# Forming one weight sum of the seven-product pairs with an accumulating DMA, and using eight such pairs per group

## The chip, the core and the metric

The kernel runs on one core of a Trainium2 chip. The core has a matrix engine (TensorE, "PE" in the profile; "PEld" is its weight load), three engines for elementwise work (VectorE, "DVE"; ScalarE, "ACT"; GpSimd, "POOL"), a queue that issues transfers (SyncE, "SP") and 16 DMA engines between HBM and the on-chip memory SBUF. TensorE adds up its results in PSUM, eight banks of 512 columns. The metric is the device time of one execution in microseconds.

## The reference

One layer of a hybrid decoder, batch 1, 256 tokens and 16 meta tokens in front, model width 4096, all in float32:

```python
h = rmsnorm(x, norm_g)
p = h @ w_in                      # 4096 x 16384: q, k, v, gate | B, C, h, z
o = stick_breaking_attention(heads(q), heads(k), heads(v))
o = group_rmsnorm(o * silu(g_attn), attn_norm_g, 16)
y = b_conv * short_conv(c_conv * h_conv, conv_w)
y = group_rmsnorm(y * silu(z_conv), conv_norm_g, 16)
return rmsnorm(x + concatenate([o, y]) @ w_out, final_norm_g)[:, 16:]
```

Almost all the arithmetic is in the two matrix products. The output keeps the 256 real tokens.

## The kernel before

**Three matmuls for one product.** TensorE multiplies in a rounded format (float32r). To keep float32 accuracy every operand is split: ScalarE casts it to the rounded format (`wh`, line 282), VectorE subtracts that from the original (`wl`, line 283), and a product is three matmuls: low x high, high x high, high x low (lines 314, 316 and 317 in `mm_p`).

**Groups and pieces.** The input projection goes through eight groups of two heads each. The list `pieces` sets the order of the work. In a group come first 16 pairs (j = 0 to 15). A pair covers two blocks of 128 rows of the weights, and has two pieces of 128 x 1024, called A and B. With W1 and W2 for the columns of q and gate, and of B and z, in the two blocks, A holds W1 of the first block and W2 of the second, B the opposite. After the pairs come 32 pieces "p" for k, v, C and h (lines 306 to 308), with the attention and convolution of the group as tasks between. After all groups the output projection follows (pieces "o", lines 705 to 707).

**Seven products in place of eight.** A pair stands for a 2 x 2 block product: two blocks of tokens times two of rows, and two sets of columns: eight block products of 512 columns, 24 matmuls. For the pairs in `SJ` (in groups 1 to 7) a scheme of the Strassen-Winograd kind does with seven products, 21 matmuls. It needs sums of the token blocks (`S`, formed once, in group 0, by `prep_x`, lines 207 to 216: four GpSimd operations, a ScalarE copy, a VectorE subtraction) and sums of the weight blocks, formed anew in each group: T (1024 columns, two sums of 512) and U (two more, written over A in its buffer). So such a pair has four pieces, A, B, T and U, of 6, 3, 6 and 6 matmuls. The products go to eight PSUM banks, and `evict_sums` (lines 479 to 491) adds them up after the last pair of `SJ`.

**What runs ahead.** At step i the program has issued loads up to piece i + 8 and splits up to piece i + 5. What holds them back are buffers: five for loaded pieces (`raw`), six for splits (`wh`, `wl`), one for T (`tt`). All loads stand in SyncE's queue in order, all casts in ScalarE's and all subtractions in VectorE's, so a waiting instruction holds what stands behind it. A scheduler orders the instructions of each engine when the program is built; it may put a load or a sum some places earlier than the code has it.

**T and U before.** When B of such a pair is split, VectorE forms T with two subtractions of 512 columns (line 293) and U with an addition and a subtraction (294, 295).

Of the kernel before, what the change touches and what calls it, by code (L numbers as in the profile page):

```python
# [37 lines left out]
WARM = 10  # L38
LOADS, SPLITS, RING = 8, 5, 6

SJ = (4, 6, 8, 10, 12, 14)


G0, CW0, AG0, CG0, NPAR = 0, 32, 80, 96, 112
# [3 lines left out]
def kernel(ctx, tc, xt, xin, xm, par, fg, w1, w2, out):  # L48
# [141 lines left out]
    def prep_x(j, parts=1):  # L190
        t = xr.pop(j)
        x = xs[j // 2][:, 2 * (j % 2):2 * (j % 2) + 2, :, :L]
        for i in range(2):
            g = pt[:, G0 + 2 * j + i:G0 + 2 * j + i + 1]
            if i or parts == 2:
                nc.vector.tensor_scalar(out=t[:, i, :], in0=t[:, i, :], scalar1=g, scalar2=None, op0=ALU.mult)
            else:
                nc.scalar.mul(out=t[:, i, :], in_=t[:, i, :], mul=g)
            if parts == 2:
                nc.scalar.copy(out=x[:, i, 0, :], in_=t[:, i, :])  # L200
                nc.vector.tensor_tensor(out=x[:, i, 1, :], in0=t[:, i, :], in1=x[:, i, 0, :].bitcast(F32), op=ALU.subtract)
        if parts == 1:
            nc.scalar.copy(out=x[:, :, 0, :], in_=t)
            nc.vector.tensor_tensor(out=x[:, :, 1, :], in0=t, in1=x[:, :, 0, :].bitcast(F32), op=ALU.subtract)
        if j not in SJ:
            return
        a11, a21 = t[:, 0, META:META + P], t[:, 0, META + P:]
        a12, a22 = t[:, 1, META:META + P], t[:, 1, META + P:]
        f = wk.tile([P, 4, P], F32, tag="u2", name=f"sf{j}", bufs=2)
        v = nc.gpsimd  # L210
        v.tensor_tensor(out=f[:, 0, :], in0=a21, in1=a22, op=ALU.add)
        v.tensor_tensor(out=f[:, 2, :], in0=a11, in1=a21, op=ALU.subtract)
        v.tensor_tensor(out=f[:, 1, :], in0=f[:, 0, :], in1=a11, op=ALU.subtract)
        v.tensor_tensor(out=f[:, 3, :], in0=a12, in1=f[:, 1, :], op=ALU.subtract)
        nc.scalar.copy(out=S[j][:, 0], in_=f)
        nc.vector.tensor_tensor(out=S[j][:, 1], in0=f, in1=S[j][:, 0].bitcast(F32), op=ALU.subtract)

# [12 lines left out]
    def load(i):  # L230
        p = pieces[i]
        if p[0] in "TU":
            return
        if p[:2] == ("A", 0) and p[2] > 0:
            load_x(p[2])
        t = wp.tile([P, 1024], F32, tag="raw", name=f"raw{i}", bufs=5)
        raws[i] = t
        if p[0] == "x":
            if p[1] < 8:
                r, c = divmod(p[1], 4)  # L240
                nc.sync.dma_start(out=t, in_=xin[r * P:(r + 1) * P, c * 1024:(c + 1) * 1024])
            else:
                nc.sync.dma_start(out=t[:, :512], in_=xm)
        elif p[0] == "m":
            nc.sync.dma_start(out=t.rearrange("p (a b) -> p a b", a=4), in_=mixd[p[1]])
        elif i < 2:
            for h in range(2):
                nc.sync.dma_start(out=t[:, 512 * h:512 * h + 512], in_=where[i][:, 512 * h:512 * h + 512])
                if i == 0 and h == 0:
                    nc.sync.dma_start(out=xr[0][:, 1:, :], in_=xt[:, 1:2, :])  # L250
        else:
            nc.sync.dma_start(out=t, in_=where[i])
# [3 lines left out]
    def split(i):  # L256
        p = pieces[i]
        if p[:2] == ("A", 0):
            prep_x(p[2], 2 if p[2] == 0 else 1)
        parts = 2 if i < 2 else 1  # L260
        if p[0] == "x":
            t = raws.pop(i)
            w = 1024 if p[1] < 8 else 512
            nc.scalar.activation(out=t[:, :w], in_=t[:, :w], func=AF.Square, accum_out=sq9[:, p[1]:p[1] + 1])
            return
        if p[0] == "m":
            t = raws.pop(i).rearrange("p (a b) -> p a b", a=4)
            h, lo = mixh[p[1]], mixl[p[1]]
            nc.scalar.copy(out=h, in_=t)
            nc.vector.tensor_tensor(out=lo, in0=t, in1=h.bitcast(F32), op=ALU.subtract)  # L270
            return
        t = sums.pop(p) if p[0] in "TU" else raws.pop(i)
        two = p[0] in "AB" and p[1] and p[2] in SJ
        w = 512 if two and p[0] == "B" else 1024
        if i in keep:
            h, lo = keep[i]
        else:
            h = wp.tile([P, 1024], F32R, tag="wh", name=f"wh{i}", bufs=RING)
            lo = wp.tile([P, 1024], F32R, tag="wl", name=f"wl{i}", bufs=RING)
        for q in range(parts):  # L280
            c = slice(q * w // parts, (q + 1) * w // parts)
            nc.scalar.copy(out=h[:, c], in_=t[:, c])  # L282
            nc.vector.tensor_tensor(out=lo[:, c], in0=t[:, c], in1=h[:, c].bitcast(F32), op=ALU.subtract)  # L283
        splits[i] = (h, lo)
        if two and p[0] == "A":
            sums[p] = t
        elif two:

            a = sums.pop(("A",) + p[1:])
            s = wp.tile([P, 1024], F32, tag="tt", name=f"t{i}", bufs=1)  # L290
            for q in range(2):
                c = slice(512 * q, 512 * q + 512)
                nc.vector.tensor_tensor(out=s[:, c], in0=a[:, c], in1=t[:, 512:], op=ALU.subtract)
            nc.vector.tensor_tensor(out=a[:, 512:], in0=a[:, 512:], in1=s[:, :512], op=ALU.add)
            nc.vector.tensor_tensor(out=a[:, :512], in0=t[:, :512], in1=a[:, 512:], op=ALU.subtract)
            sums[("T",) + p[1:]], sums[("U",) + p[1:]] = s, a


    psum = {}
# [179 lines left out]
    def evict_sums(g):  # L479

        cq = wk.tile([P, 2, 512], F32, tag="cq", name=f"cq{g}")
        cb = wk.tile([P, 2, 512], F32, tag="cb", name=f"cb{g}")
        gr[g] = dict(cq=cq, cb=cb)
        if g == 0:
            return
        p1, p5, p7, p6 = (psum.pop((g, q)) for q in (P1, P5, P7, P6))
        A.copy(out=cq[:, 0], in_=p1)
        V.tensor_tensor(out=cb[:, 0], in0=p6, in1=cq[:, 0], op=ALU.add)
        V.tensor_tensor(out=cq[:, 1], in0=p7, in1=cb[:, 0], op=ALU.add)
        V.scalar_tensor_tensor(out=cb[:, 0], in0=p5, scalar=-1.0, in1=cb[:, 0], op0=ALU.mult, op1=ALU.add)  # L490
        V.scalar_tensor_tensor(out=cb[:, 1], in0=p5, scalar=-1.0, in1=cq[:, 1], op0=ALU.mult, op1=ALU.add)

    def evict(g):
        s = gr[g]
# [186 lines left out]
    def load_res(nb):  # L681
        c, w = cols(nb)
        for t in range(2):
            nc.sync.dma_start(out=res[t][:, c:c + w], in_=xin[t * P:(t + 1) * P, c:c + w])
        f = fgs["pool"].tile([P, 512], F32, tag="fg", name=f"fg{nb}", bufs=2)
        nc.sync.dma_start(out=f[:, :w], in_=fg[:, c:c + w].broadcast_to([P, w]))
        fgs[nb] = f

# [169 lines left out]
```

## Time and profile before

| | |
|---|---|
| time, median of 3 runs | 1837.21 us (1837.15 to 1838.44) |
| profiled execution | 1838.6 us, span from first to last instruction 1836.7 us |
| granted TensorE clock | 0.997 of full speed |
| HBM | read 354.48 MB, written 7.86 MB, 197 GB/s over the span |
| group 0: pairs | about 7 to 96 us |
| groups 1 to 7: one each | some 182 us, of which the pairs take about 83 |
| output projection and end | from 1472.8 us |

The profile is one execution. "Busy" is the time in which an engine worked on at least one instruction; matmuls overlap, so their durations add up to more than that. A row such as `L283 DVE TENSOR_TENSOR wl<-raw,wh` names the line of the kernel, the engine, the operation and the tiles written and read. In the rows in order of time the first two columns are the start and the duration in microseconds, and a bracket says how long the engine stood idle before and what released it.

### The profile page before, as it was taken

The numbers are of one execution on the slowest core, as the hardware profiler recorded it, in microseconds if no ns is written. First come the engines' busy times: TensorE is split into PE (matmuls) and PEld (weight loads), VectorE is DVE, ScalarE is ACT, GpSimd is POOL, SyncE is SP. The second block draws the span as 40 slices with busy tenths as digits, with TensorE's granted clock in tenths as the row PEclk, the third lists the DMA queues.
The fourth block names the chain that finished last, engine by engine and source line by source line (L and its number), as shares of the span: only waits on it lengthen the run. The fifth ranks groups of instructions, "written<-read, shape, count | busy, mean of one in ns | idle before, by whom it ended". The sixth has DMA issues, their size and how long they took to land.

```text
span 1836.7 us, 29147 instructions
## 1 busy us (share of the span) xinstructions
PE 1822.2 (99%) x11196; PEld 1646.2 (90%) x11196; DVE 1243.0 (68%) x1855; ACT 1036.9 (56%) x1593; POOL 103.0 (6%) x144
## 2 busy tenths in 40 slices
PE   9999999999999999999999999999999999999997
PEld 7899889988998899889988998899889988888887
DVE  6776687668666866786668667866786764555553
ACT  6766556655665566556656565656566654444442
POOL 1210001000100010001000100010001000000000
PEclk9999999999999999999999999999999999999999
DMA  8865566556545654565557555655475686666563
GB/s 307 300 211 170 169 214 201 170 168 219 194 170 171 217 197 165 176 218 188 172 172 227 182 172 166 230 183 174 162 234 191 203 303 216 197 199 203 198 210 115
DMA packets 106844, 364.26 MB, mean 198 GB/s; under 512 B 11984, under 2 KB 16848, under 8 KB 106704
## 3 DMA queue, kind: packets, MB, share of 16 engines
q1 hardware_dynamic: 102672, 358.72, 58.8%
q10 hardware_dynamic: 4032, 3.67, 0.6%
q8 instruction: 88, 1.44, 0.3%
q14 instruction: 52, 0.43, 0.1%
HBM read 354.48 MB, written 7.86 MB: 197 GB/s over the span
## 4 chain that ended last, share of the span: by engine, by line
PE 98%; ACT 1%; DVE 1%; DMA 1%; issue 0%; DVEq 0%; SPq 0%; ACTq 0%
PE mm L306 14%; PE mm L308 13%; PE mm L307 13%; PE P L317 12%; PE P L314 12%; PE P L316 12%; PE mo L705 6%; PE mo L706 6%; PE mo L707 6%; PE z L573 0%; PE po L619 0%; DMA raw<-mixd 0%; PE z L572 0%; PE po L615 0%; PE mxc L541 0%
## 5 line engine op out<-in xcount | busy, mean ns | idle before, releaser
L283 DVE TENSOR_TENSOR wl<-raw,wh 128x1024 fp32r<-128x1024 f32 (+1 forms) x682 | 801.7, 1193 | 389.1 <-ACT wh L282 386.8
L282 ACT CAST wh<-raw 128x1024 fp32r<-128x1024 f32 (+1 forms) x682 | 684.3, 1021 | 617.6 <-PE mm L307 195.4
L306 PE MATMUL mm<-xs,wh 128*128 128x258 f32 (+1 forms) x2048 | 588.1, 287 | 0.0
L308 PE MATMUL mm<-xs,wl 128*128 128x258 f32 (+1 forms) x2048 | 581.8, 284 | 0.0
L307 PE MATMUL mm<-xs,wh 128*128 128x258 f32 (+1 forms) x2048 | 581.8, 284 | 0.0
L306 PEld LDWEIGHTS mm<-xs,wh 128*128 128x128 f32 x2048 | 385.5, 188 | 2.8
L307 PEld LDWEIGHTS mm<-xs,wh 128*128 128x128 f32 x2048 | 385.6, 188 | 0.9
L308 PEld LDWEIGHTS mm<-xs,wl 128*128 128x128 f32 x2048 | 385.5, 188 | 0.0
L314 PE MATMUL P<-wh,xs 128*128 128x512 f32 x814 | 318.7, 392 | 1.8 <-ACT wh L282 1.8
L317 PE MATMUL P<-wl,xs 128*128 128x512 f32 x814 | 317.6, 390 | 0.0
L316 PE MATMUL P<-wh,xs 128*128 128x512 f32 x814 | 317.4, 390 | 0.0
L705 PE MATMUL mo<-wh,mixl 128*128 128x512 f32 (+1 forms) x560 | 206.3, 368 | 0.0
L706 PE MATMUL mo<-wh,mixh 128*128 128x512 f32 (+1 forms) x560 | 206.1, 368 | 0.0
L707 PE MATMUL mo<-wl,mixh 128*128 128x512 f32 (+1 forms) x560 | 206.0, 368 | 0.0
L314 PEld LDWEIGHTS P<-wh,xs 128*128 128x128 f32 x814 | 153.2, 188 | 33.1 <-ACT wh L282 2.0
L317 PEld LDWEIGHTS P<-wl,xs 128*128 128x128 f32 x814 | 153.3, 188 | 32.2
L316 PEld LDWEIGHTS P<-wh,xs 128*128 128x128 f32 x814 | 153.2, 188 | 31.2
L707 PEld LDWEIGHTS mo<-wl,mixh 128*128 128x128 f32 x560 | 105.6, 189 | 17.6
L705 PEld LDWEIGHTS mo<-wh,mixl 128*128 128x128 f32 x560 | 105.6, 189 | 17.4
L706 PEld LDWEIGHTS mo<-wh,mixh 128*128 128x128 f32 x560 | 105.6, 189 | 17.2
L314 PE MATMUL P<-wh,sum 128*128 128x512 f32 x168 | 65.4, 389 | 0.0
L317 PE MATMUL P<-wl,sum 128*128 128x512 f32 x168 | 65.4, 389 | 0.0
(212 smaller groups left out, 1294.7 us busy)
## 6 DMA issues: line engine op xcount, KB each, us to landing
raw<-w SPq DMA_DIRECT2D x638, 512.0 KB, 3.7
raw<-xin SPq DMA_DIRECT2D x8, 512.0 KB, 5.2
xr<-xt SPq DMA_DIRECT2D x15, 272.0 KB, 5.5
raw<-mixd SPq DMA_DIRECT2D x7, 512.0 KB, 3.8
res<-xin SPq DMA_DIRECT2D x14, 256.0 KB, 6.4
out<-res SPq DMA_DIRECT2D x4, 512.0 KB, 3.5
mixd<-mfh ACTq DMA_DIRECT2D x14, 128.0 KB, 2.5
mixd<-mfc ACTq DMA_DIRECT2D x14, 128.0 KB, 4.8
```

Of the source, the lines that this page charges most:

```text
L282: nc.scalar.copy(out=h[:, c], in_=t[:, c])
L283: nc.vector.tensor_tensor(out=lo[:, c], in0=t[:, c], in1=h[:, c].bitcast(F32), op=ALU.subtract)
L306: nc.tensor.matmul(out=o, lhsT=h, rhs=x[:, 0, s:], start=k == 0, stop=False)
L307: nc.tensor.matmul(out=o, lhsT=h, rhs=x[:, 1, s:], start=False, stop=False)
L308: nc.tensor.matmul(out=o, lhsT=lo, rhs=x[:, 0, s:], start=False, stop=k == KC - 1)
L314: nc.tensor.matmul(out=o, lhsT=a[1], rhs=h, start=key not in begun, stop=False)
L316: nc.tensor.matmul(out=o, lhsT=a[0], rhs=h, start=False, stop=False)
L317: nc.tensor.matmul(out=o, lhsT=a[0], rhs=lo, start=False, stop=last)
L705: T.matmul(out=o, lhsT=ml, rhs=h, start=m == 0, stop=False)
L706: T.matmul(out=o, lhsT=mh, rhs=h, start=False, stop=False)
L707: T.matmul(out=o, lhsT=mh, rhs=lo, start=False, stop=m == UNITS - 1)
```

## The change

T is no longer computed by VectorE. When A of a seven-product pair is loaded, SyncE also copies the second half of B (512 columns) twice into a buffer of 1024 columns, straight from HBM, and GpSimd issues a transfer that adds A, read from HBM again, to that buffer. [...] VectorE still forms U, with two additions (lines 297 and 298), when T is split. B's loaded piece therefore stays in its buffer until then. T has two buffers instead of one; the tail's gain vectors move into them. `SJ` has eight pairs instead of six, with a plain pair after every two. The scratch area for GpSimd's transfers grows from 256 to 1024 bytes.

```diff
-SJ = (4, 6, 8, 10, 12, 14)
+SJ = (4, 5, 7, 8, 10, 11, 13, 14)
...
-        v.tensor_tensor(out=f[:, 0, :], in0=a21, in1=a22, op=ALU.add)
+        v.tensor_tensor(out=f[:, 0, :], in0=a21, in1=a22, op=ALU.subtract)
...
-        v.tensor_tensor(out=f[:, 3, :], in0=a12, in1=f[:, 1, :], op=ALU.subtract)
+        v.tensor_tensor(out=f[:, 3, :], in0=a12, in1=f[:, 1, :], op=ALU.add)
...
+        if p[0] == "A" and p[1] and p[2] in SJ:
+
+            s = wp.tile([P, 1024], F32, tag="tt", name=f"t{i}", bufs=2)
+            nc.sync.dma_start(out=s.rearrange("p (a b) -> p a b", a=2),
+                              in_=where[i + 1][:, 512:].unsqueeze(1).broadcast_to([P, 2, 512]))
+            nc.gpsimd.dma_start(out=s, in_=where[i], accum_op=ALU.add)
+            sums[("T",) + p[1:]] = s
...
-        if two and p[0] == "A":
+        if two:
             sums[p] = t
-        elif two:
-
-            a = sums.pop(("A",) + p[1:])
-            s = wp.tile([P, 1024], F32, tag="tt", name=f"t{i}", bufs=1)
-            for q in range(2):
-                c = slice(512 * q, 512 * q + 512)
-                nc.vector.tensor_tensor(out=s[:, c], in0=a[:, c], in1=t[:, 512:], op=ALU.subtract)
-            nc.vector.tensor_tensor(out=a[:, 512:], in0=a[:, 512:], in1=s[:, :512], op=ALU.add)
-            nc.vector.tensor_tensor(out=a[:, :512], in0=t[:, :512], in1=a[:, 512:], op=ALU.subtract)
-            sums[("T",) + p[1:]], sums[("U",) + p[1:]] = s, a
+        elif p[0] == "T":
+
+            a, b = sums.pop(("A",) + p[1:]), sums.pop(("B",) + p[1:])
+            nc.vector.tensor_tensor(out=a[:, 512:], in0=a[:, 512:], in1=t[:, :512], op=ALU.add)
+            nc.vector.tensor_tensor(out=a[:, :512], in0=b[:, :512], in1=a[:, 512:], op=ALU.add)
+            sums[("U",) + p[1:]] = a
...
-        V.scalar_tensor_tensor(out=cb[:, 0], in0=p5, scalar=-1.0, in1=cb[:, 0], op0=ALU.mult, op1=ALU.add)
-        V.scalar_tensor_tensor(out=cb[:, 1], in0=p5, scalar=-1.0, in1=cq[:, 1], op0=ALU.mult, op1=ALU.add)
+        V.tensor_tensor(out=cb[:, 0], in0=p5, in1=cb[:, 0], op=ALU.subtract)
+        V.tensor_tensor(out=cb[:, 1], in0=p5, in1=cq[:, 1], op=ALU.subtract)
...
-        f = fgs["pool"].tile([P, 512], F32, tag="fg", name=f"fg{nb}", bufs=2)
+        f = wp.tile([P, 1024], F32, tag="tt", name=f"fg{nb}", bufs=2)
...
-    nc = bacc.Bacc("TRN2", target_bir_lowering=False, num_devices=1, dynamic_dma_scratch_size=256)
+    nc = bacc.Bacc("TRN2", target_bir_lowering=False, num_devices=1, dynamic_dma_scratch_size=1024)
```

The order of the built program shows what this moves. First VectorE, in group 1, from one plain pair through the seven-product pair behind it. The number after `wl`, `raw` and `t` is the piece (`wl105` to `wl108` are A, B, T and U of pair 12), the number after that only makes the name unique. Before:

```order
L283 TENSOR_TENSOR wl103_2605<-raw103_2555,wh103_2604 128x1024
L293 TENSOR_TENSOR t106_2643<-raw105_2584,raw106_2602 128x512 x2
L283 TENSOR_TENSOR wl104_2621<-raw104_2572,wh104_2620 128x1024
L283 TENSOR_TENSOR wl105_2631<-raw105_2584,wh105_2630 128x1024
L283 TENSOR_TENSOR wl106_2640<-raw106_2602,wh106_2639 128x512
L294 TENSOR_TENSOR raw105_2584<-raw105_2584,t106_2643 128x512
L283 TENSOR_TENSOR wl107_2657<-t106_2643,wh107_2656 128x1024
L295 TENSOR_TENSOR raw105_2584<-raw106_2602,raw105_2584 128x512
L283 TENSOR_TENSOR wl108_2669<-raw105_2584,wh108_2668 128x1024
```

And after, pairs 12 (plain, `wl109` and `wl110`), 13 (111 to 114) and the start of 14 (from 115):

```order
L290 TENSOR_TENSOR wl109_2686<-raw109_2645,wh109_2685 128x1024
L290 TENSOR_TENSOR wl110_2696<-raw110_2657,wh110_2695 128x1024
L290 TENSOR_TENSOR wl111_2706<-raw111_2671,wh111_2705 128x1024
L290 TENSOR_TENSOR wl112_2718<-raw112_2683,wh112_2717 128x512
L297 TENSOR_TENSOR raw111_2671<-raw111_2671,t111_2668 128x512
L290 TENSOR_TENSOR wl113_2730<-t111_2668,wh113_2729 128x1024
L298 TENSOR_TENSOR raw111_2671<-raw112_2683,raw111_2671 128x512
L290 TENSOR_TENSOR wl114_2742<-raw111_2671,wh114_2741 128x1024
L290 TENSOR_TENSOR wl115_2758<-raw115_2715,wh115_2757 128x1024
L297 TENSOR_TENSOR raw115_2715<-raw115_2715,t115_2712 128x512
L298 TENSOR_TENSOR raw115_2715<-raw116_2727,raw115_2715 128x512
L290 TENSOR_TENSOR wl116_2776<-raw116_2727,wh116_2775 128x512
```

Of the four sums two are left on VectorE, and in pair 14 both stand ahead of the split of B, right behind A's split: T of that pair must be there by then.

Second, SyncE's queue at the same place: before, only loads of pieces:

```order
L252 DMA raw103_2555<-w1 128x1024
L252 DMA raw104_2572<-w1 128x1024
L252 DMA raw105_2584<-w1 128x1024
L252 DMA raw106_2602<-w1 128x1024
L252 DMA raw109_2637<-w1 128x1024
```

After, with the broadcasts of B's half (`t`) of pairs 11, 13 and 14 among the loads:

```order
L259 DMA raw102_2555<-w1 128x1024
L237 DMA t105_2584<-w1 128x2x512
L259 DMA raw105_2587<-w1 128x1024
L259 DMA raw106_2599<-w1 128x1024
L259 DMA raw109_2645<-w1 128x1024
L237 DMA t111_2668<-w1 128x2x512
L259 DMA raw110_2657<-w1 128x1024
L259 DMA raw111_2671<-w1 128x1024
L259 DMA raw112_2683<-w1 128x1024
L237 DMA t115_2712<-w1 128x2x512
```

Each broadcast has come in ahead of its pair's own loads, or one or two places earlier. GpSimd's queue, which held no transfer, has the accumulating ones in the same order; those of the next group's first two pairs (`t161`, `t165`) stand ahead of the gates of the group that is running:

```order
L239 DMA t115_2712<-w1 128x1024
L239 DMA t161_4096<-w1 128x1024
L239 DMA t165_4189<-w1 128x1024
L513 TENSOR_TENSOR cq1_2865<-cq1_2865,sgh1_2943 128x2x128 x2
L513 TENSOR_TENSOR cb1_2866<-cb1_2866,sgc1_2948 128x2x128
```

Third, ScalarE in group 0, around pair 11 (`xr11`) and 12: before, pair 11 has no token sums, so its scaled tokens (`xs`) are followed by the casts of its weights at once:

```order
L198 ACTIVATE xr11_585<-xr11_585,pt_83 128x272
L203 CAST xs5_128<-xr11_585 128x2x272
L282 CAST wh29_645<-raw29_587 128x1024
L282 CAST wh30_663<-raw30_616 128x1024
L264 ACTIVATE raw31_622,sq9_119<-raw31_622 128x1024
```

After, the copy of GpSimd's sums (`sum11`) stands ahead of them:

```order
L198 ACTIVATE xr11_594<-xr11_594,pt_83 128x272
L203 CAST xs5_128<-xr11_594 128x2x272
L215 CAST sum11_140<-sf11_654 128x512
L289 CAST wh29_661<-raw29_596 128x1024
L289 CAST wh30_679<-raw30_625 128x1024
L271 ACTIVATE raw31_631,sq9_119<-raw31_631 128x1024
```

Pairs 5, 7, 11 and 13 get such a copy, pairs 6 and 12 lose theirs. At pair 14 alone the cast of A stands ahead of it.

## The prediction

> **What bounds the kernel now.** I read the head of the page first, then what TensorE waits for, then its rows one by one.
>
> ```profile
> span 1836.7 us, 29147 instructions
> PE 1822.2 (99%) x11196; PEld 1646.2 (90%) x11196; DVE 1243.0 (68%) x1855; ACT 1036.9 (56%) x1593; POOL 103.0 (6%) x144
> PE P L314 <- ACT wh L282: 1.8, 1, 1.8
> ```
>
> TensorE is busy for 1822 of 1837 us, and the list of its waits has one of 1.8 us at the start. So time is gained by giving TensorE fewer matmuls, and lost where another engine lets it run dry. The duration of a matmul is not what one costs, as the rows in order of time show:
>
> ```profile
> L314 PE MATMUL P<-wh,xs 128*128 128x512 f32 x814 | 318.7, 392 | 1.8 <-ACT wh L282 1.8
> 599.79 0.39 PE L314 MATMUL P<-wh,xs 128*128 128x512 f32 x1
> ...
> 608.63 0.39 PE L314 MATMUL P<-wh,xs 128*128 128x512 f32 x1
> ```
>
> Each lasts 0.39 us, but 39 of them start between 599.79 and 608.63: one every 0.227 us, because they overlap. A pair of the plain kind has 24 such matmuls (5.44 us), a seven-product pair 21 (4.76 us).
>
> How far the other engines run ahead decides what a stall costs. In group 3 (of 0 to 7), for a T piece (columns: start, duration):
>
> ```profile
> 608.21 1.22 DVE L283 TENSOR_TENSOR wl<-t,wh 128x1024 fp32r<-128x1024 f32 x1
> 611.23 2.36 DVE L283 TENSOR_TENSOR wl<-raw,wh 128x1024 fp32r<-128x1024 f32 x2 [1.19 <-ACT wh L282]
> 613.50 1.28 DVE L293 TENSOR_TENSOR t<-raw,raw 128x512 f32<-128x512 f32 x2
> 614.71 2.37 DVE L283 TENSOR_TENSOR wl<-raw,wh 128x1024 fp32r<-128x1024 f32 x2
> 615.43 0.39 PE L314 MATMUL P<-wh,sum 128*128 128x512 f32 x1
> ```
>
> The split of T ends at 609.43, its matmuls start at 615.43: a lead of 6.0 us. The starts also give VectorE's real price: two of 1024 columns take 2.27 us (1.14 each), two of 512 take 1.21 (0.60 each).
>
> **The change, part by part.** *Matmuls.* Two more pairs of each of seven groups become seven-product pairs: 14 x 3 = 42 matmuls fewer, as the built program has them (10934 rows against 10976). 42 x 0.227 = **-9.5 us**. Taking 0.39 us for each would give 16.4, which is wrong for rows that overlap.
>
> *VectorE and ScalarE in a group.* The repeating piece is now two seven-product pairs and a plain one: 2 x 4.76 + 5.44 = 14.96 us of TensorE. VectorE does eight splits of 1024 columns (9.1 us), two of 512 and four additions (3.6 us): 12.7 us, 85%. Gone are the two subtractions of line 293. What that is worth depends on whether VectorE holds anything up in this stage (first row):
>
> ```profile
> 592.00:632.00 40.00, 40.00 (x179) 33.10 (x178) 35.03 (x41) 22.40 (x24) 0.00 (x0) 1.00 0.66 206
> 60.00:75.00 15.00, 15.00 (x68) 12.43 (x67) 10.75 (x14) 12.12 (x19) 2.25 (x4) 1.00 0.87 322
> 1500.00:1510.00 10.00, 10.00 (x45) 8.26 (x44) 4.84 (x4) 4.08 (x4) 0.00 (x0) 1.00 1.03 399
> ```
>
> (Columns: stretch, then busy time of PE, weight load, VectorE, ScalarE, GpSimd, then clock, share of the DMA engines, GB/s.) VectorE had 35.03 of 40 us, 88%; so taking work from it gains nothing, and it does not become the bound. ScalarE has 22.40 of 40 and gets only one more split per new T and U. Both count as nothing, as long as T is there in time. The four scalar forms that become tensor forms (lines 490 and 491) cost the same on VectorE.
>
> *DMA rate.* In 14.96 us there were six loads of 512 KB, there are now ten transfers (two broadcasts, two accumulations more): 10 x 0.524 MB / 14.96 us = 350 GB/s, where the stage has 206 now. The engines moved 399 over ten microseconds (third row), so 350 fits, but not with much room.
>
> *The chain to T.* This is the new wait. SyncE copies the second half of B twice into the buffer, GpSimd waits for that landing and issues the accumulating transfer, and ScalarE and VectorE wait for this second landing in their own queues: behind them stand the splits of U, of B and of the next pairs. There are two buffers; the next broadcast into one waits until its T is split. What a landing costs (columns: KB each, us from issue to landing), in the stage now, in the first group, and in the tail's densest stretch:
>
> ```profile
> raw<-w SPq DMA_DIRECT2D x16, 512.0 KB, 4.0
> ...
> raw<-w SPq DMA_DIRECT2D x15, 512.0 KB, 6.0
> ...
> raw<-w SPq DMA_DIRECT2D x5, 512.0 KB, 6.1
> ```
>
> The broadcast lies between 4.0 (206 GB/s) and 6.1 (392 to 399); 350 GB/s is nearest to the loaded rows, so 6.0. No accumulating transfer is in this trace. It moves as many bytes as a load and reads its target besides: not below 4.0, and two loaded landings, 12.0, as the upper end. I take 6.0, the loaded row of its size. C, from the broadcast's issue to T being there, is then **12.0 us**, between 8 and 18.
>
> How long may C be? In each group T5, T8, T11 and T14 use one buffer in turn (the numbers are pairs), T4, T7, T10 and T13 the other; T4 and T5 are fetched long before they are needed, since the built program puts the next group's first two on the queues right after T14's. From the end of T5's split to TensorE's start on B14 stand 195 matmuls, 44.2 us. T5's own lead is shorter than the 6.0 above: the ring of six lets its split begin when A4's matmuls are done, and 24 matmuls (5.4 us) less the split (about 2.3) leave 3.1. Ahead of B14's split VectorE must do the two additions and that split, 3 x 0.60 = 1.8. And after each T comes, two additions, B's split and T's, 2.95 us, pass before the buffer is free, twice. 44.2 + 3.1 - 1.8 - 5.9 = 39.6 for three chains: **C may be 13.2 us**. At 12.0 it is hidden: **0 us**, by a margin of 1.2. Each microsecond over costs 3 x 7 = 21 us. On GpSimd's queue the accumulations for the next group's pairs 4 and 5 now stand ahead of the gates of this group; the gates need pair 15's sums, some 8 us of TensorE later than T14, so they wait for nothing new: 0.
>
> *Token sums in the first group.* Here the change has a second price. A pair with sums holds ScalarE longer:
>
> ```profile
> 44.14 1.06 ACT L264 ACTIVATE raw<-raw 128x1024 f32<-128x1024 f32 x1 [1.14 <-DMA raw<-xin]
> ...
> 48.14 0.62 ACT L215 CAST sum<-sf 128x512 fp32r<-128x512 f32 x1 [1.75 <-POOL sf L214]
> 48.67 1.99 ACT L282 CAST wh<-raw 128x1024 fp32r<-128x1024 f32 x2
> ...
> 56.85 0.52 ACT L198 ACTIVATE xr<-xr,pt 128x272 f32<-128x272 f32 x1 [0.69 <-DMA xr<-xt]
> ```
>
> ScalarE stands 1.75 us for GpSimd's sums and then 0.53 on their copy, 2.28 in all. And it has little lead left there:
>
> ```profile
> 64.69 2.00 ACT L282 CAST wh<-raw 128x1024 fp32r<-128x1024 f32 x2
> 65.77 2.36 DVE L283 TENSOR_TENSOR wl<-raw,wh 128x1024 fp32r<-128x1024 f32 x2 [0.23 <-PE P L316]
> 66.91 1.06 ACT L264 ACTIVATE raw<-raw 128x1024 f32<-128x1024 f32 x1 [0.22 <-DMA raw<-xin]
> ...
> 68.53 0.39 PE L314 MATMUL P<-wh,xs 128*128 128x512 f32 x1
> ```
>
> A of pair 11 is split at about 67.0 and needed at 68.53: 1.5 us ahead. Up to pair 11 there were four pairs with sums, there are now six: 4.56 us more, of which the DMA waits in these rows (1.14 + 0.69 + 0.22 = 2.05) can take part. 4.56 - 2.05 - 1.5 = 1.0 us of stall; 0 if more of it is hidden, 3.1 if the DMA waits stay. Pair 14 does not add to it: in the new order its A is cast ahead of its sums. I take **+1.0 us**.
>
> *Moved buffers and a larger scratch area* change addresses alone. The tail's gain vectors now use T's buffers, free since the last group: 0.
>
> *Sum.* -9.5 + 1.0 = -8.5 us. The profiled execution has a span of 1836.7 and a time of 1838.6, 1.9 us around the span; it becomes 1828.2 and 1830.1. The median of the runs is 1837.2, 1.4 below that execution; less 8.5 it gives **1828.7**.
>
> [...] No run here shows an accumulating transfer yet.
>
> **Rivals.** *T comes late (slower).* The accumulation holds the DMA engines longer than a load, because it also reads what it adds to. Halfway between one loaded landing and two it lands in 9.0 us; C is 15.0, 1.8 over, and 1.8 x 21 = 38 us: **1866.5**. It decides from C = 13.2. For it: 1.2 us of margin is little beside an operation that no row prices. Against it: 4.0 us is what a landing takes now, and the accumulation has a queue of its own beside SyncE's. [...]
>
> *The DMA engines are full.* With 322 GB/s, as in the first group, ten transfers need 16.3 us, 1.3 over in each three pairs; a group has 54.4 / 14.96 = 3.6 of these, 4.8 us, of which 3.1 of lead is spent: 1.7 x 7 = 12, **1841**. Against it: the first group is not at its limit at a share of 0.87, and the tail moves 399.
>
> *More is gained than the pitch says.* If the matmuls' 0.39 us were time, 16.4 - 1.0 = 15.4: **1822**. The rows 0.227 apart speak against it.
>
> **How the numbers follow.** The forecast gets 0.56; with its own bounds (0 to 3.1 in the first group, C just over for some of the chains) it reaches from 1826 to 1832. T late gets 0.28, full engines 0.08, more gained 0.02, and 0.06 is left for a C only some tenths over, 1832 to 1841. A measurement of this kernel can tell about 0.2% from no change, 3.7 us. Faster: 0.56 + 0.02 = 0.58. Slower: 0.28 and half of 0.08, 0.32. Same: the rest, 0.10. The range goes from 1825 to 1867: it leaves out the upper half of T late (C to 18 would be 4.8 x 21 = 101 us) and the 1822, 0.16 in all.
>
> **What would show it.** Right: 10934 matmuls, TensorE's waits near zero in groups 1 to 7, broadcast and accumulation landing together within 13 us, VectorE still waiting for casts that wait for TensorE. T late: waits of TensorE for casts, these for the accumulating transfer, about the same sum in each of seven groups. Full engines: a DMA share near 1 between pairs 4 and 15 and late loads of A and B as well. The first group: gaps of TensorE between 50 and 90 us, about 1. The forecast fails first at the landing of the accumulation.

## The result and the profile after

| | before | after |
|---|---|---|
| time, median of 4 runs each | 1837.18 us (1837.12 to 1838.44) | 1924.57 us (1916.31 to 1926.45) |
| ratio, 95% interval | | 1.0462, 1.0448 to 1.0476 |
| profiled execution, its span | 1838.6, 1836.7 us | 1923.4, 1921.4 us |
| granted TensorE clock | 0.997 | 0.986 |

The change makes the kernel 4.6% slower; the forecast was 0.5% faster, and the time lies outside its range. From the page of the changed kernel, the busy times, the queue of GpSimd's transfers and the chain that ended last:

```profile
PE 1844.0 (96%) x11154; PEld 1650.2 (86%) x11154; DVE 1241.4 (65%) x1829; ACT 1057.3 (55%) x1623; POOL 147.6 (8%) x208
...
q0 software_dynamic: 8064, 29.36, 8.5%
...
PE 81%; DMA 10%; DVE 4%; issue 3%; ACT 2%; ACTq 0%; POOL 0%; DVEq 0%; SPq 0%; POOLq 0%
```

TensorE has its 42 matmuls less and is yet busy for longer, and a tenth of the chain is now DMA, which had 1% before. The list of waits (engine, line, what it waited for: total us, times, longest) tells where:

```profile
ACT wh L289 <- DMA raw<-w: 70.8, 48, 5.8
ACT wh L289 <- DMA t<-w: 69.2, 25, 6.9
...
PE mm L309 <- DVE cq L492: 34.3, 7, 6.3
...
PE P L320 <- DVE wl L290: 26.9, 38, 4.7
```

ScalarE waits 69.2 us for T's transfers, TensorE 26.9 us for late splits inside the pairs, and 34.3 us seven times, once per group, at its first plain piece (line 309), there for VectorE's evictions of the product banks. Before, TensorE had none of these waits.

I took the start of each piece's first matmul on TensorE, from all matmul records of the traces, and summed the differences of the pieces' times against before. Of the 84.8 us, **36.3** lie in the pairs of all groups up to B of pair 15 (where 9.5 less and 1.0 more were due, so some 45 are lost), **35.5** between B of pair 15 and the first plain piece, **12.8** in that first plain piece, and 0.2 in all other plain pieces. This table, made in the same way for every run, is what the experiments below are read by. The four columns of differences are microseconds in one execution, the profiled one, which lies up to 6 us from the median in the last column:

| run | pairs, to B of 15 | wait for first plain piece | first plain piece | other plain pieces | median time |
|---|---|---|---|---|---|
| changed kernel | +36.3 | +35.5 | +12.8 | +0.2 | 1924.57 |
| later_first_two | +36.5 | +15.6 | +3.7 | 0.0 | 1893.32 |
| plain_copy | +7.6 | +32.5 | +11.5 | 0.0 | 1886.04 |
| three_buffers | -1.0 | +33.7 | +13.1 | +5.3 | 1889.64 |
| eight_by_vector | +23.1 | +22.7 | +11.9 | +0.4 | 1893.92 |
| three_buffers_free_banks | +1.1 | +5.2 | +0.4 | +5.0 | 1847.47 |
| three_buffers_free_304 | -0.2 | +3.6 | +0.5 | +3.1 | 1848.96 |
| eight_by_vector_free_banks | +27.0 | +1.7 | +0.6 | +0.1 | 1865.28 |
| six_pairs_transfer | -0.1 | +1.5 | +0.2 | 0.0 | 1838.93 |
| changed_free_banks | +31.9 | +1.1 | +0.3 | +0.9 | 1878.76 |
| before_288 | +9.9 | +0.4 | +0.2 | +5.0 | 1854.68 |
| half_by_vector_free_banks | -8.5 | 0.0 | 0.0 | 0.0 | 1829.58 |
| seven_pairs_three_buffers | -1.6 | +2.9 | +0.3 | 0.0 | 1837.36 |

**Inside the pairs.** One chain to a T, in order of time, group 3 of the changed kernel (start, duration, engine and line): the split of T11, which frees the buffer, the broadcast into it, the accumulation, and the cast of T14:

```profile
650.79 1.22 DVE L290 TENSOR_TENSOR wl<-t,wh 128x1024 fp32r<-128x1024 f32 x1
652.03 0.38 SPq L237 DMA_DIRECT2D t<-w  x1
659.99 0.87 POOL L239 DMA_DIRECT2D t<-w  x1 [8.30 <-DMA t<-w]
666.42 1.04 ACT L289 CAST wh<-t 128x1024 fp32r<-128x1024 f32 x1 [2.58 <-PE P L320]
```

The buffer is free at 652.01, T lands at 666.27 and ScalarE's cast of it starts at 666.42 (the bracket names TensorE, which finished a matmul at that moment; the place in the ring that the cast needs had been free since about 661): 14.4 us, which is also the median of all the chains that wait for a buffer (the longest 18.4). The view of the transfers has 6.8 us for the broadcast, which ends here at 659.3, and 7.4 for the accumulation (KB each, median us to landing):

```profile
t<-w SPq DMA_DIRECT2D x56, 512.0 KB, 6.8
t<-w POOLq DMA_DIRECT2D x56, 512.0 KB, 7.4
```

**At the end of the pairs.** The same group, a little later: ScalarE's casts and VectorE's work around the evictions (lines 491 and 492), and TensorE's last matmul of pair 15 and first of the plain piece:

```profile
675.11 1.05 ACT L289 CAST wh<-raw 128x1024 fp32r<-128x1024 f32 x1 [2.85 <-DMA raw<-w]
678.63 1.04 ACT L289 CAST wh<-raw 128x1024 fp32r<-128x1024 f32 x1 [2.48 <-DMA raw<-w]
...
677.19 0.39 PE L320 MATMUL P<-wl,xs 128*128 128x512 f32 x1
683.41 0.56 PE L309 MATMUL mm<-xs,wh 128*128 128x272 f32 x1 [5.84 <-DVE cq L492]
...
679.71 1.23 DVE L290 TENSOR_TENSOR wl<-raw,wh 128x1024 fp32r<-128x1024 f32 x1 [2.30 <-ACT wh L289]
680.85 0.68 DVE L491 TENSOR_TENSOR cb<-P,cq 128x512 f32<-128x512 f32 x1
...
682.59 0.68 DVE L492 TENSOR_TENSOR cq<-P,cb 128x512 f32<-128x512 f32 x1
```

The first plain piece waits for nothing of its own: it was split before 675. It waits for a PSUM bank, and the evictions that free it stand on VectorE behind the split at 679.71, that of the group's third plain piece, whose load lands only at 678.5. The same two evictions before:

```profile
639.74 0.68 DVE L488 TENSOR_TENSOR cb<-P,cq 128x512 f32<-128x512 f32 x1
...
641.47 0.68 DVE L489 TENSOR_TENSOR cq<-P,cb 128x512 f32<-128x512 f32 x1
```

There TensorE had begun pair 15 at 638.55 and came to the first plain piece at 643.99, 1.8 us after the second eviction. After, pair 15 begins at 671.97, so the evictions come 8.9 us behind it instead of 1.2.

**The clock.** Windows of the changed kernel behind that idle time (stretch, length, busy times of PE, PEld, DVE, ACT, POOL, then clock, DMA share, GB/s):

```profile
677.40:683.30 5.90, 0.17 (x1) 0.00 (x0) 3.60 (x6) 4.22 (x4) 0.28 (x1) 0.97 1.03 337
683.30:686.70 3.40, 3.29 (x16) 3.32 (x17) 3.40 (x5) 1.65 (x3) 0.74 (x1) 0.55 1.02 367
686.70:690.00 3.30, 3.30 (x29) 3.30 (x28) 3.30 (x5) 2.37 (x4) 2.42 (x2) 1.00 0.59 212
```

For 3.4 us after it the granted clock is 0.55 and 16 matmuls are recorded, then 29 in as much time at full clock. That is the 12.8 us of the first plain pieces: 1.4 to 2.6 in each group. Three more such spells, of 3.4 us at a clock of 0.50, lie inside the pairs of groups 1 and 2, behind idle times of 2.09, 4.73 and 2.88 us; by an estimate from the clock (3 x 3.4 us at half speed) they make some 5 of the 45 us lost there.

### The profile page after: what moved, and what is told of

Same layout as the page of the kernel before. It is cut to its first block, busy times and chain, and to the rows that moved or that the text cites. A ratio compares the mean times of both kernels' runs of the same rounds, so it can differ in the third digit from the quotient of the medians.

```text
span 1921.4 us, 29466 instructions
## 1 busy us (share of the span) xinstructions
PE 1844.0 (96%) x11154; PEld 1650.2 (86%) x11154; DVE 1241.4 (65%) x1829; ACT 1057.3 (55%) x1623; POOL 147.6 (8%) x208
## 3 DMA queue, kind: packets, MB, share of 16 engines
q0 software_dynamic: 8064, 29.36, 8.5%
## 4 chain that ended last, share of the span: by engine, by line
PE 81%; DMA 10%; DVE 4%; issue 3%; ACT 2%; ACTq 0%; POOL 0%; DVEq 0%; SPq 0%; POOLq 0%
PE mm L309 13%; PE mm L310 13%; PE mm L311 13%; PE P L320 7%; PE P L317 7%; PE P L319 7%; PE mo L710 6%; PE mo L708 6%; PE mo L709 6%; DMA t<-w 6%; DMA raw<-w 4%; DVE wl L290 3%; ACT wh L289 1%; PE z L576 0%; PE po L622 0%
## 5 line engine op out<-in xcount | busy, mean ns | idle before, releaser
L290 DVE TENSOR_TENSOR wl<-raw,wh 128x1024 fp32r<-128x1024 f32 (+1 forms) x696 | 810.7, 1183 | 407.7 <-ACT wh L289 406.3
L309 PE MATMUL mm<-xs,wh 128*128 128x258 f32 (+1 forms) x2048 | 594.6, 290 | 34.3 <-DVE cq L492 34.3
L310 PE MATMUL mm<-xs,wh 128*128 128x258 f32 (+1 forms) x2048 | 587.2, 287 | 0.0
L309 PEld LDWEIGHTS mm<-xs,wh 128*128 128x128 f32 x2048 | 391.3, 191 | 39.6 <-issue 37.1
L310 PEld LDWEIGHTS mm<-xs,wh 128*128 128x128 f32 x2048 | 391.3, 191 | 0.6
L320 PE MATMUL P<-wl,xs 128*128 128x512 f32 x744 | 293.4, 395 | 23.2 <-DVE wl L290 23.2
L317 PE MATMUL P<-wh,xs 128*128 128x512 f32 x744 | 292.6, 393 | 3.4 <-ACT wh L289 3.4
L319 PE MATMUL P<-wh,xs 128*128 128x512 f32 x744 | 290.2, 390 | 0.0
L320 PEld LDWEIGHTS P<-wl,xs 128*128 128x128 f32 x744 | 140.2, 188 | 61.5 <-DVE wl L290 32.8
L317 PEld LDWEIGHTS P<-wh,xs 128*128 128x128 f32 x744 | 140.5, 189 | 34.4 <-ACT wh L289 5.8
L319 PEld LDWEIGHTS P<-wh,xs 128*128 128x128 f32 x744 | 140.3, 189 | 28.5
L289 ACT CAST wh<-t 128x1024 fp32r<-128x1024 f32 x56 | 58.7, 1049 | 88.6 <-DMA t<-w 69.2
L320 PE MATMUL P<-wl,sum 128*128 128x512 f32 x224 | 90.5, 404 | 3.7 <-DVE wl L290 3.7
```

The lines of the kernel that those rows point to most:

```text
L309: nc.tensor.matmul(out=o, lhsT=h, rhs=x[:, 0, s:], start=k == 0, stop=False)
L310: nc.tensor.matmul(out=o, lhsT=h, rhs=x[:, 1, s:], start=False, stop=False)
L317: nc.tensor.matmul(out=o, lhsT=a[1], rhs=h, start=key not in begun, stop=False)
L319: nc.tensor.matmul(out=o, lhsT=a[0], rhs=h, start=False, stop=False)
L320: nc.tensor.matmul(out=o, lhsT=a[0], rhs=lo, start=False, stop=last)
```

## The experiments

Three causes were open: the chain to T, longer than its two buffers allow (theory 1); the DMA engines, full with adding packets (theory 2); and the next group's first two broadcasts, which stand on SyncE's queue ahead of the plain pieces' loads and wait there for a buffer (theory 3). Against all three stood that eight pairs might be too many in themselves.

**later_first_two.** The transfers of pairs 4 and 5 are asked for late.

```diff
-        if p[0] == "A" and p[1] and p[2] in SJ:
+        if p[0] == "A" and p[1] and p[2] in SJ[2:]:
+            form(i)
...
+        load_raw(i, p)
+        if p[0] == "A" and p[1] and p[2] in (1, 2):
+            j = SJ[p[2] - 1]
+            form(pieces.index(("A", p[1], j)), raws[i])
...
+            if after is not None:
+                nc.scalar.copy(out=s[:, :1], in_=after[:, :1])
```

> The broadcasts of a group's first two T (pairs 4 and 5) are held back until the A pieces of pairs 1 and 2 have landed (ScalarE copies one column of those into T's buffer first), so that they no longer stand on SyncE's queue ahead of the loads of the plain pieces; all else as in the changed kernel. If SyncE's queue is what delays the first plain piece, the waits of TensorE there (35.5 us over seven groups) and the half clock behind them (12.8) go, and the time falls by about 48 to some 1876 us; the loss inside pairs 4 to 14 (45.8) stays. If the plain pieces are late only because T13 and T14 are late on ScalarE and VectorE, the time stays above 1915 us.

Measured 1893.32 us, ratio 1.029 (1.0266 to 1.0314). The wait and the first plain piece fall from 48.3 to 19.3 us, the pairs stay at 36.5. So the early transfers of the next group carry 29 of the 48, not all: neither side of the expectation. Something makes the evictions late without them.

It is not SyncE's queue that makes the difference, as theory 3 had it. In both kernels, and in every group, the third plain piece's load is issued 0.03 us after the split of U14 ends, which leaves its buffer free. The two views of the transfers around that issue in group 3, first of the changed kernel, then of this run:

```profile
raw<-w SPq DMA_DIRECT2D x1, 512.0 KB, 7.9
```

```profile
raw<-w SPq DMA_DIRECT2D x1, 512.0 KB, 3.8
```

In the changed kernel T4's accumulation and T5's broadcast of the next group are in flight beside that load, and the DMA engines' share is 1.02 until it lands; here neither is, and the share is 0.83. The medians of the seven groups are 7.7 and 3.3 us, and 3.4 before.

**plain_copy.** The same transfer without the addition; the second half of B is then missing from T.

```diff
-            nc.gpsimd.dma_start(out=s, in_=where[i], accum_op=ALU.add)
+            nc.gpsimd.dma_start(out=s, in_=where[i])
```

> GpSimd's transfer overwrites the buffer instead of adding to it; the second half of B is then missing from T, so the output is another one, but every instruction, queue and wait is the same. If the adding itself (a packet of 4096 bytes at 328 ns instead of 159) is the cause, by the length of the chain or by the load on the DMA engines, the second transfer lands in about 6 us instead of 7.4, the chain takes 12 to 13, and the time falls to about 1830 us. If SyncE's queue costs its 48 us whether T comes late or not, the time is about 1878 us.

Measured 1886.04 us, ratio 1.0263 (1.0248 to 1.0279). GpSimd's queue on its page (packets, MB, share of the DMA engines), and the second transfer in the view of the transfers:

```profile
q0 software_dynamic: 8064, 29.36, 4.6%
```

```profile
t<-w POOLq DMA_DIRECT2D x56, 512.0 KB, 6.1
```

It lands in 6.1 us instead of 7.4. A packet takes 4.6% x 16 engines x 1888.5 us / 8064 = 0.172 us, with the addition 8.5% x 16 x 1921.4 / 8064 = 0.324 (of the packets of 4096 bytes alone the medians are 0.159 and 0.328). The chain, counted as above, goes from 14.4 to 13.1 us, and of the 45 us lost inside the pairs 29 come back. The wait at the first plain piece stays (32.5): it doesn't hang on the addition.

**three_buffers.** T goes through three buffers in turn.

```diff
-XROW = 320
+XROW = 288
...
-            s = wp.tile([P, 1024], F32, tag="tt", name=f"t{i}", bufs=2)
+            k = 8 * p[1] + SJ.index(p[2]) - 8
+            s = (xp.tile([P, 1024], F32, tag="tx", name=f"t{i}") if k % 3 == 2 else
+                 wp.tile([P, 1024], F32, tag="tt", name=f"t{i}", bufs=2))
```

> T gets three buffers in turn instead of two (the rows of the split x are padded to 288 instead of 320 to make room). Each buffer then comes round every four and a half pairs, 22 us instead of 15, and the next group's first broadcasts find a free buffer, so they hold SyncE no more. If the chain of 14.2 us in 13.2 is the cause, nothing is late: about 1830 us. If the DMA engines are full (twelve loads' worth in 14.96 us), a third buffer adds no bandwidth: the loss inside the pairs, 46 us, stays and only the wait at the first plain piece can go: 1876 us or more.

Measured 1889.64 us, ratio 1.0281 (1.0264 to 1.0298). TensorE's waits, and a window of 40 us in the pairs of one group:

```profile
PE mm L311 <- DVE cq L494: 32.2, 7, 6.2
PE P L319 <- ACT wh L291: 2.3, 1, 2.3
```

```profile
600.00:640.00 40.00, 40.00 (x178) 32.88 (x177) 32.08 (x35) 24.11 (x27) 4.36 (x5) 1.00 0.97 302
```

In groups 1 to 7 no wait is left inside the pairs, with the same transfers and the DMA engines at a share of 0.97: theory 2 falls as the bound inside the pairs, theory 1 holds for this part. The wait at the first plain piece is there undiminished.

**eight_by_vector.** Eight pairs, and VectorE forms T by two additions as soon as B is split. (In the changed kernel T is a sum, where it was a difference before; to give the same products, the token sums and two of the additions after the last pair have other signs.)

```diff
+TX = ()
...
-        if p[0] == "A" and p[1] and p[2] in SJ:
+        if p[0] == "A" and p[1] and p[2] in TX:
...
+            if p[0] == "B" and p[2] not in TX:
+                a = sums[("A",) + p[1:]]
+                s = wp.tile([P, 1024], F32, tag="tt", name=f"t{i}", bufs=2)
+                for q in range(2):
+                    c = slice(512 * q, 512 * q + 512)
+                    nc.vector.tensor_tensor(out=s[:, c], in0=a[:, c], in1=t[:, 512:], op=ALU.add)
+                sums[("T",) + p[1:]] = s
```

> Eight pairs per group, but T is formed by two additions on VectorE again, with no transfers. If the transfers are the cause of the whole loss, 42 matmuls less bring 9.5 us, and VectorE, which has 6.7 us of work for a pair with sums and 2.46 for a plain one, needs 63.4 us for pairs 4 to 15 against 60.0 of TensorE: up to 3.4 us of wait in each of seven groups, 1828 to 1852 us. If eight pairs are too many in themselves (splits, token sums, order), the time is near 1900 us or above it also here.

Measured 1893.92 us, ratio 1.0304 (1.0289 to 1.032): far above the 1852, and near the 1900 that was expected if eight pairs are too many in themselves. Without any transfer there are still 34.6 us at the first plain piece, so its cause is in the eight pairs.

The times of the splits show it. Pairs 13 and 14 now stand side by side. The split of U14 ends 5.9 us ahead of pair 15's start before, and 2.6, 1.3, 1.3 and 0.3 us ahead in three_buffers, the changed kernel, later_first_two and this run (group 3). In all seven groups of these five runs ScalarE's cast of U14 starts 0.1 us after VectorE's second addition for U14 has ended. In group 3 of the changed kernel:

```profile
667.07 0.69 DVE L298 TENSOR_TENSOR raw<-raw,raw 128x512 f32<-128x512 f32 x1
667.88 2.94 ACT L289 CAST wh<-raw 128x1024 fp32r<-128x1024 f32 x3 [0.41 <-DVE raw L298]
```

In the changed kernel the two additions wait for T14 (landed at 666.27, the first starts at 666.35); in this run they stand behind VectorE's other sums and splits, which leave it idle for 0.8 of the 13 us ahead. The third plain piece is loaded into the buffer that U14 leaves, its split waits for that load, and the evictions stand behind that split.

In this run two things differ. Its third load lands after 3.2 us, and it is the fourth plain piece's split, waiting for its load, that holds the second eviction (in six of the seven groups, as in later_first_two). And the wait at the first plain piece is put down to a cast:

```profile
PE mm L317 <- ACT wh L290: 21.6, 7, 3.5
```

In this program the first two matmuls of the group's fifth plain piece stand on TensorE's queue ahead of the first piece, and wait for the fifth's cast and so for its load. The second eviction ends between 0.6 us before these matmuls start and 0.6 after, so the bank alone would have made nearly the same wait.

Six of the runs that follow test this by putting the third plain piece's split behind the evictions. The edit has two parts, which were only tried together: a copy makes that split wait for the last eviction, and U14's matmuls and the evictions come ahead of the loads and splits of their step:

```diff
+        if p[0] == "p" and p[1][0] % 2 == 0 and p[1][0] and p[1][1] == 0 and p[2] == 2:
+            nc.scalar.copy(out=h[:, :1], in_=gr[p[1][0] // 2]["cb"][:, 1, :1])
...
+        last = 0 <= i < n1 and pieces[i][0] == "U" and pieces[i][2] == SJ[-1]
+        if last:
+            mm_in(i)
+            evict_sums(pieces[i][1])
```

**three_buffers_free_banks** and **three_buffers_free_304** (the same with `XROW = 304`).

> Three buffers as in the run before, and the group's third plain piece is split behind the sums' evictions (ScalarE first copies one column of the last eviction's result into the split's target), where it stood ahead of them on VectorE. If that split, which waits for its load, is what keeps the banks from being freed, the waits at the first plain piece (33.7 us) and the half clock behind them (13.1) go: 1889.6 less 46.8, about 1843 us. If the banks are late for another reason (the products themselves, or ScalarE's copy of P1), the time stays near 1890 us.

> The same with the rows of the split x padded to 304 instead of 288. With 288 each group's plain pieces took 0.65 us longer (5.3 us in all); if that is the padding's work and 304 doesn't have it, about 1838 us; if it comes from the third buffer's transfers, 1843 us as with 288.

Measured 1847.47 us, ratio 1.0052 (1.0037 to 1.0067), and 1848.96, ratio 1.0059 (1.0044 to 1.0074). Both are above what was expected (1843; 1838 or 1843). The wait and the first plain piece fall from 46.8 to 5.6 and 4.1 us. What is left over is not waits: the pairs gain almost nothing where 9.5 were due, and the plain pieces take 5.0 and 3.1 us more.

**eight_by_vector_free_banks.**

> Eight pairs with T formed by VectorE and no transfers, the third plain piece's split behind the evictions. The same mechanism without any transfer: the waits at the first plain piece (22.7) and the half clock there (11.9) go, 1893.9 less 34.6, about 1859 us. If the banks are late because VectorE as a whole is behind, at most half of it goes: 1876 us or more.

Measured 1865.28 us, ratio 1.0148 (1.0131 to 1.0165). 32.3 of the 34.6 us go, with no transfer in the kernel, and the fifth piece's matmuls no longer stand in front; so late evictions don't need the transfers. The pairs lose 27.0 + 8.5 = some 36 us. Pairs 4 to 14 of group 3, first here, then in half_by_vector_free_banks below, where nothing is lost (the third busy time is VectorE's):

```profile
590.95:651.12 60.17, 56.51 (x243) 44.32 (x242) 50.34 (x59) 32.34 (x38) 0.00 (x0) 1.00 0.52 171
581.17:635.71 54.54, 54.54 (x243) 45.16 (x242) 51.02 (x56) 35.90 (x40) 3.48 (x4) 1.00 0.87 266
```

VectorE is busy for 84% of the time here and for 94% there, so its work in total is not the limit. ScalarE's casts of T and U wait 25.7 us of the 60.2 for VectorE's sums: the loss is in the order in which the two engines wait for each other. No run tested which step of it.

**changed_free_banks.** The changed kernel with that edit alone.

> The changed kernel (two buffers) with one thing else: the group's third plain piece is split behind the sums' evictions. If that split, late with its load, is the whole of the wait at the first plain piece, the 35.5 us there and the 12.8 of half clock behind them go, 1924.6 less 48, about 1876 us, with the loss inside the pairs as it was. If SyncE's queue is a cause of its own, beside that split, the first plain piece or its neighbours still wait for their loads: 1890 us or more.

Measured 1878.76 us, ratio 1.0227 (1.0212 to 1.0243). TensorE's waits:

```profile
PE P L322 <- DVE wl L292: 16.7, 38, 1.9
PE P L319 <- ACT wh L291: 7.6, 10, 2.1
...
PE mm L311 <- DVE cq L494: 0.6, 1, 0.6
```

48.3 us at the first plain piece become 1.4, though the next group's transfers are asked for as before: they are one of the things that make that load late, and the load costs time nearly only through the split that stands ahead of the evictions. The loss inside the pairs stays.

**six_pairs_transfer.** The changed kernel with the old list of pairs.

```diff
-SJ = (4, 5, 7, 8, 10, 11, 13, 14)
+SJ = (4, 6, 8, 10, 12, 14)
```

> The changed kernel with the six pairs of before: T formed by the transfers, but no pairs with sums side by side and no matmul less. Each buffer comes round every four pairs, 20.4 us, so by the theory of the chain nothing is late inside the pairs; U of pair 14 is split with the lead it had before, so the banks are freed in time: 1837 to 1840 us. If the broadcasts asked for ahead of the plain pieces, or the adding packets, cost their time whatever the pairs are, the waits at the first plain piece come back: up to 48 us more, 1885 us.

Measured 1838.93 us, ratio 1.0008 (0.9999 to 1.0018). The transfers alone cost nothing, and taking two sums of four from VectorE brings nothing.

**before_288.** The kernel before with `XROW = 288`.

> The kernel before with the rows of the split x padded to 288 instead of 320, and nothing else. If the padding is what took 0.62 us in each group's plain pieces and about 1.0 in its pairs (gain of 0.36 to 0.40 where 1.36 was due), about 12 us more than before: 1850 us. If those came from the third buffer's transfers, no change: 1837.5 us.

Measured 1854.68 us, ratio 1.009 (1.0076 to 1.0103), some 5 us above the expected. So the remainder of the runs with three buffers was their narrower rows of x: 9.9 and 5.0 us here, 9.6 (1.1 + 8.5) and 5.0 in three_buffers_free_banks. Two of the matmul groups (last column but one: mean ns) have 399 and 396 where 392 and 390 stood before:

```profile
L314 PE MATMUL P<-wh,xs 128*128 128x512 f32 x814 | 324.7, 399 | 2.0 <-ACT wh L282 2.0
L317 PE MATMUL P<-wl,xs 128*128 128x512 f32 x814 | 322.0, 396 | 0.0
```

**half_by_vector_free_banks.** Every second T by VectorE (`TX = (5, 8, 11, 14)` in the edit of eight_by_vector), and the split behind the evictions.

> Eight pairs, two buffers, third plain piece's split behind the evictions; pairs 5, 8, 11 and 14 have T from the transfers, pairs 4, 7, 10 and 13 by VectorE's two additions. Nine loads' worth instead of twelve in 14.96 us, so the chain should land in 12 to 13 us, within its 13.2; VectorE has 6.7 + 5.5 + 2.46 = 14.7 us of work for three pairs in 14.96. If both fit, 1837.5 less 9.5 and 1 or 2 of small waits, 1828 to 1832 us. If VectorE at 98% leaves no lead to the splits, part of the 36 us that eight pairs by VectorE alone lost inside the pairs comes back: 1835 to 1850 us.

Measured 1829.58 us (1828.65 to 1830.5), ratio to before 0.9954 (0.9942 to 0.9967): **faster than both kernels**, by 0.5% against before. TensorE's waits for splits, its only ones of more than 0.4 us behind the first matmuls of the program, and then, in order of time, the split of T4, T8's broadcast and the split of T5:

```profile
PE P L327 <- ACT wh L292: 1.8, 2, 1.6
...
PE P L330 <- DVE wl L293: 1.0, 2, 0.5
```

```profile
576.23 1.22 DVE L293 TENSOR_TENSOR wl<-t,wh 128x1024 fp32r<-128x1024 f32 x1 [2.29 <-ACT wh L292]
577.48 0.38 SPq L238 DMA_DIRECT2D t<-w  x1
...
584.18 1.23 DVE L293 TENSOR_TENSOR wl<-t,wh 128x1024 fp32r<-128x1024 f32 x1 [1.75 <-ACT wh L292]
```

I had expected a shorter chain, and it isn't: broadcast and accumulation land in 5.8 and 8.5 us. But the broadcast goes into the buffer that T4, formed by VectorE, has left at 577.45, 8 us before T5's split ends at 585.41, and VectorE's next T takes T5's.

**seven_pairs_three_buffers.** `SJ = (4, 5, 7, 8, 10, 12, 14)`, the third buffer in the place of the eighth pair's token sums, the split behind the evictions.

> Seven pairs (4, 5, 7, 8, 10, 12, 14) with the transfers and three buffers; the third buffer takes the place of the eighth pair's token sums, so that the rows of x keep their 320; third plain piece's split behind the evictions. 21 matmuls less are 4.8 us, group 0 costs 0.5, and the first plain piece kept 0 to 5 us of waits in the run with three buffers and eight pairs: 1833 to 1838 us. If the transfers cost more than that (loads landing late beside them), 1840 us or more.

Measured 1837.36 us, ratio 0.9999 (0.999 to 1.0008). No difference, at the upper end of the expectation: 4.8 us less of matmuls, and 3.2 at the first plain pieces and 3.2 in the pairs (2.8 of them in group 1) given back.

## Why the prediction was wrong

- **Matmuls, -9.5: right.** In half_by_vector_free_banks each of groups 2 to 7 is 1.36 us shorter in its pairs, 6 matmuls x 0.227. The rival with 16.4 was wrong.
- **Token sums in the first group, +1.0: right.** +0.56 in the changed kernel, +1.06 in half_by_vector_free_banks, and 0.56 to 1.47 in the seven runs with eight pairs and rows of 320. Both terms together, -8.5, are what half_by_vector_free_banks measures: -8.5 in its pairs, -8.4 between the medians.
- **"taking work from it gains nothing": right** for six pairs (six_pairs_transfer). With eight pairs it does matter who forms T: with all of it on VectorE the pairs lose 36 us (eight_by_vector_free_banks), with half of it none.
- **"At 12.0 it is hidden: 0 us": wrong, the first step that failed.** C measured 14.4 us. The accumulation takes 7.4 instead of 6.0, the broadcast 6.8 (6.6 in the chains that wait) instead of 6.0, and 0.7 us from the broadcast's landing to GpSimd's issue, which the sum left out, come on top (medians, which need not add up). The waits for T, with the half clock behind some of them, cost some 45 us. The limit of 13.2 was too high as well: with a median of 13.1, in plain_copy, the pairs lose 16 us already. The chains spread about their medians (12.2 to 18.4 in the changed kernel), and the prediction compared one length with one limit. Its price of 21 us for each microsecond is near the 29 us between these two runs for 1.4 us of chain; but changed_free_banks, with 15.2, loses 40, so the price is not settled. The rival "T comes late" had this mechanism and 38 us for it at C = 15.0.
- **What no step had: the end of the pairs, 48 us.** The sum took pair 13 as 3 matmuls less, and priced nothing behind the split of B14 but the gates, at 0. With sums in pair 13 VectorE's second addition for U14, and with it U14's split, the load into U14's buffer and the evictions behind that load, come later, and the 1.8 us that the evictions had to spare are gone; changed_free_banks takes back 46.9 of the 48.3 by the order around the evictions alone. Of T4 and T5 the prediction says only that they "are fetched long before they are needed". That their transfers run just when the plain pieces' loads do, and make the third of these land in 7.7 us instead of 3.4 before, it put at nothing; later_first_two prices it at 29 of the 48.
- **The rival "the DMA engines are full": wrong as the bound inside the pairs.** A share of 0.97 in three_buffers lets TensorE run without a wait. Behind the pairs the loaded engines do count, by the third plain piece's load (in group 3 it lands after 7.9 us at a share of 1.02, and after 3.8 at 0.83 in later_first_two). What the addition costs a transfer: a packet takes 0.324 us where the copying one takes 0.172 (plain_copy), and the landing 7.4 us where it takes 6.1.

In three_buffers the third plain piece's load is also issued 0.03 us after U14's split ends, and lands after 8.5 us (median), at a DMA share of 1.03 in group 3: there too the time is lost between issue and landing, beside full DMA engines, and not in a wait on SyncE's queue. What stays open is why U14's split itself is late in three_buffers, where T14 landed in time.

## What to carry to other kernels

When a change makes pieces of work shorter, buffers counted in pieces cover less time: follow the last piece of a stage through the sums it needs, its load buffer and the instructions queued behind it, to whatever the next stage needs first. A chain through two transfers and two engines is to be summed with the time between them, and its longest case, not its middle one, held against the time until its buffer comes round; one buffer more, or every second T formed elsewhere, was worth more here than faster transfers (inside the pairs -1.0 us against before in three_buffers and -8.5 in half_by_vector_free_banks, but +7.6 in plain_copy). An instruction that frees a bank shouldn't stand behind one that waits for a load: in changed_free_banks the order around the evictions alone took back 46.9 of 48.3 us.

## What the runs showed of the hardware

- **Half the clock after short idle times.** Over all runs, 25 of 25 first plain pieces that TensorE began 2.9 to 6.5 us late took 1.4 to 2.6 us longer; of 15 that began 1.0 to 2.75 us late, 14 took at most 0.12 longer (the other one, 2.36 late, 1.64). In the changed kernel a granted clock of 0.50 to 0.53 over 3.4 us stands behind idle times of 3.17 us (ahead of group 1's first plain piece) and of 2.88 and 2.09 (inside the pairs of groups 2 and 1); behind one of 2.26 (inside the pairs of group 7) it stayed at 1.00.
- **Narrower rows of x cost time here.** The same 272 columns in rows padded to 288 instead of 320 cost 0.9% (before_288): 0.62 us in each group's plain pieces and 1.13 in its pairs. Rows of 304 (three_buffers_free_304) took 0.39 in the plain pieces, and the pairs lost 1.2 (a gain of 0.15 where 1.36 was due). The edit also moves the addresses of what is allocated behind x; whether the stride or the place does it was not tested.
